# Group softmax on one core: stores moved from SyncE's ring to GpSimd's queue, loads left on SyncE's ring

One Trainium2 chip, one core. The metric is device microseconds of a whole execution, the median of several runs; a profile's span is the same execution seen from inside and is some 2 us shorter. A run is called slow here when it is over 1.5% above the fastest of its kernel. "Landing" is the moment when all sixteen completions of a transfer have arrived (the trace has 2048 of them for 128 DMAs).

## The reference

The input x is 4 x 4096 x 4352 in float32. Each row of 4352 falls into 8 groups of 544, and each group gets its own softmax:

```python
x_g = x.reshape(B, N, 8, 544)
x_g = x_g - x_g.max(axis=-1, keepdims=True)
exp = np.exp(x_g)
out = exp / exp.sum(axis=-1, keepdims=True)
```

285.2 MB are read and 285.2 MB are written.

## The kernel before

A tile is 256 rows, two per partition: 128 x 8704 numbers, 4352 KB. There are 64 tiles, five buffers, and all is done in place. VectorE takes the negated maxima of a row (eight groups at once), ScalarE eight exponentials with their sums, VectorE the reciprocals and the product. Loads and stores stand in one order on one ring, that of SyncE:

```python
def take(engine, sem, n=1):
    engine.sem_inc(sem, -n).wait_op(sem, n, "sem-ge")
# ... (row, vector_max, vector_scale, scalar_exp)
def load(t, source):
    nc.sync.dma_start(out=bufs[t % NT][:, :], in_=source).then_inc(landed[t % NT], 16)

def store(t, target):
    take(nc.sync, scaled, R)
    nc.sync.dma_start(out=target, in_=bufs[t % NT][:, :]).then_inc(stored[t % NT], 16)

def step(t, source, target):
    store(t, target)
    take(nc.sync, stored[(t - 1) % NT], 16)
    load(t + AHEAD, source)          # AHEAD = 4

for t in range(AHEAD):
    load(t, xt[t])
nc.sync.sem_inc(stored[NT - 1], 16)
with nc.sync.Fori(0, ring_turns) as u:
    for t in range(NT):
        step(t, turn_in[u, t], turn_out[u, t])
# ... (the last four tiles, and the waits for the last five stores)
```

VectorE's order: the maximum of row s+1 stands before the scaling of row s.

## Time and profile before

| | before |
|---|---|
| time, median of the first 3 runs (4 with the one beside the changed kernel) | 1329.14 us (1329.29 us) |
| span of the profiled run | 1326.8 us |
| DMA: mean over the span, steady part | 430 GB/s, 433 GB/s |
| VectorE busy | 91% |
| last store landed / end | 1325.5 us / 1326.8 us |

Two more lines of the kernel before, from the instructions at its last source lines (operation and count, then duration in ns as min/median/max, then start of the first and the last in us):

```profile
L56 SPq COMPARE_BRANCH  x1: 43/43/43, 1325.6 to 1325.6; - x1
```

```profile
L169 POOLq DRAIN  x3: 34/41/82, 0.7 to 1326.6; - x3
```

SyncE's branch at 1325.6 us comes right after its wait for the last store. The second line is GpSimd's DRAIN, an instruction of the program's fixed closing and not of the kernel's text; the longest takes 82 ns. In the packed trace the first of the three (41 ns) ran already at 0.7 us, because GpSimd has no work in this kernel; the other two (82 and 34 ns) stand at the end. Between the landing and the end lie 1.3 us.

### The profile page before, as it was taken

The numbers are of one execution on the slowest core, as the hardware profiler recorded it, in microseconds if no ns is written. First come the engines' busy times: TensorE is split into PE (matmuls) and PEld (weight loads), VectorE is DVE, ScalarE is ACT, GpSimd is POOL, SyncE is SP. The second block draws the span as 40 slices with busy tenths as digits, with TensorE's granted clock in tenths as the row PEclk, the third lists the DMA queues.
The fourth block names the chain that finished last, engine by engine and source line by source line (L and its number), as shares of the span: only waits on it lengthen the run. The fifth ranks groups of instructions, "written<-read, shape, count | busy, mean of one in ns | idle before, by whom it ended". The sixth has DMA issues, their size and how long they took to land. (4 is left out here: it accounts for less than half of the span.)

```text
span 1326.8 us, 3155 instructions
## 1 busy us (share of the span) xinstructions
DVE 1207.7 (91%) x384; ACT 764.4 (58%) x2049; POOL 0.2 (0%) x4
## 2 busy tenths in 40 slices
DVE  5999999999898898998988989889899898998984
ACT  3666565655565555655655556555565555655652
POOL 0000000000000000000000000000000000000000
DMA  9999999999999999999999999999999999999998
GB/s 403 419 431 433 429 430 430 436 433 429 431 433 436 433 431 430 435 435 436 431 431 433 436 433 433 430 432 436 435 433 429 433 436 436 431 430 433 435 435 358
DMA packets 18435, 570.46 MB, mean 430 GB/s; under 512 B 2048, under 2 KB 2048, under 8 KB 2048
## 3 DMA queue, kind: packets, MB, share of 16 engines
q1 hardware_dynamic: 18432, 570.43, 99.7%
q14 instruction: 3, 0.02, 0.0%
HBM read 285.21 MB, written 285.21 MB: 430 GB/s over the span
## 5 line engine op out<-in xcount | busy, mean ns | idle before, releaser
L82 ACT ACTIVATE xt<-xt,mx 128x544 f32<-128x544 f32 x1024 | 751.3, 734 | 539.2 <-DVE mx L63 539.2
L63 DVE TENSOR_REDUCE mx<-xt 128x8 f32<-128x4352 f32 x128 | 599.1, 4681 | 94.8 <-DMA xt<-in_x_dram 94.8
L72 DVE TENSOR_TENSOR xt<-xt,rs 128x4352 f32<-128x4352 f32 x128 | 600.6, 4692 | 4.4
L82 ACT ACTIVATION_READ_ACCUMULATOR xt<-xt,mx 128x1 f32 x1024 | 191.0, 187 | 0.0
L69 DVE RECIPROCAL rs<-sm 128x8 f32<-128x8 f32 x128 | 24.6, 193 | 2.6 <-ACT xt L82 2.6
L121 ACT ACT_TABLE_LOAD x1 | 1.3, 1283 | 0.9 <-SPq L49 0.9
L158 POOL MEMSET const-bfloat16-1.0<- 128x1 bf16 x1 | 0.1, 101 | 0.0
L158 POOL MEMSET const-uint8-127<- 128x1 uint8 x1 | 0.1, 101 | 0.0
L158 POOL MEMSET const-float32-0.0<- 128x1 f32 x1 | 0.1, 98 | 0.2 <-issue 0.2
L158 POOL MEMSET const-float32-1.0<- 128x1 f32 x1 | 0.1, 98 | 0.0
## 6 DMA issues: line engine op xcount, KB each, us to landing
xt<-in_x_dram SPq DMA_DIRECT2D x64, 4352.0 KB, 30.6
out_dram<-xt SPq DMA_DIRECT2D x64, 4352.0 KB, 40.3
```

The costliest lines, as they stand in the source:

```text
L63: i = nc.vector.reduce_max(out=mx[:, s, :], in_=row(s), axis=X, negate=True)
L69: nc.vector.reciprocal(out=rs[:, s, :], in_=sm[:, s, :]).wait_op(exp_done, s + 1, "sem-ge").then_inc(rec_done, 1)
L72: nc.vector.tensor_tensor(out=xr, in0=xr, in1=rs[:, s, :].unsqueeze(2).to_broadcast([P, G, Dg]), op=mybir.AluOpType.mult,).wait_op(rec_don ...
L82: i = nc.scalar.activation(out=xr[:, g, :], in_=xr[:, g, :], func=Exp, bias=mx[:, s, g:g + 1], scale=1.0, accum_out=sm[:, s, g:g + 1],)
L121: nc.scalar.preload_act_table(Exp)
L158: nc = _bacc.Bacc("TRN2", target_bir_lowering=False, num_devices=1)
```

## The change

Its intent: take the stores, and with them the waits for the computation, out of the order of the loads. SyncE only loads, up to five tiles ahead; GpSimd only stores, from a loop of 12 turns of five tiles and four tiles after it. The whole diff:

```diff
--- before.py
+++ after.py
@@ -19,7 +19,6 @@
     R = 2
     NT = 5
     S = R * NT
-    AHEAD = NT - 1
     xf = x.flatten_outer_dims()
     of = out.flatten_outer_dims()
     N, D = xf.shape
@@ -27,15 +26,13 @@
     nt = N // (P * R)
     nr = nt * R
     turns = (nr - 1) // S
-    ring_turns = (nt - AHEAD) // NT
+    ring_turns = nt // NT
     steps = ring_turns * NT
     f32 = mybir.dt.float32
     X = mybir.AxisListType.X
     Exp = mybir.ActivationFunctionType.Exp
     xt = xf.rearrange("(t p r) d -> t p (r d)", p=P, r=R)
     ot = of.rearrange("(t p r) d -> t p (r d)", p=P, r=R)
-    turn_in = xf[AHEAD * P * R:(AHEAD + steps) * P * R, :].rearrange(
-        "(u b p r) d -> u b p (r d)", b=NT, p=P, r=R)
     turn_out = of[:steps * P * R, :].rearrange("(u b p r) d -> u b p (r d)", b=NT, p=P, r=R)
 
     landed = [tc.alloc_semaphore(f"landed{b}") for b in range(NT)]
@@ -95,28 +92,23 @@
     def load(t, source):
         nc.sync.dma_start(out=bufs[t % NT][:, :], in_=source).then_inc(landed[t % NT], 16)
 
+    for t in range(nt):
+        if t >= NT:
+            nc.sync.wait_ge(stored[t % NT], 16 * (t // NT))
+        load(t, xt[t])
+    for t in range(nt - NT, nt):
+        nc.sync.wait_ge(stored[t % NT], 16 * (t // NT + 1))
+
+
     def store(t, target):
-        take(nc.sync, scaled, R)
-        nc.sync.dma_start(out=target, in_=bufs[t % NT][:, :]).then_inc(stored[t % NT], 16)
+        take(nc.gpsimd, scaled, R)
+        nc.gpsimd.dma_start(out=target, in_=bufs[t % NT][:, :]).then_inc(stored[t % NT], 16)
 
-    def step(t, source, target):
-        store(t, target)
-        take(nc.sync, stored[(t - 1) % NT], 16)
-        load(t + AHEAD, source)
-
-    for t in range(AHEAD):
-        load(t, xt[t])
-    nc.sync.sem_inc(stored[NT - 1], 16)
-    with nc.sync.Fori(0, ring_turns) as u:
+    with nc.gpsimd.Fori(0, ring_turns) as u:
         for t in range(NT):
-            step(t, turn_in[u, t], turn_out[u, t])
+            store(t, turn_out[u, t])
     for t in range(steps, nt):
-        if t + AHEAD < nt:
-            step(t, xt[t + AHEAD], ot[t])
-        else:
-            store(t, ot[t])
-    for t in range(nt - NT, nt):
-        nc.sync.wait_ge(stored[t % NT], 16)
+        store(t, ot[t])
 
     nc.scalar.preload_act_table(Exp)
     with nc.scalar.Fori(0, turns):
```

## The prediction

> **What bounds the kernel now.** I read the page's shares first, then the queues, then stretches of the middle and the end, then the waits and the issues in order of time. The page, busy rows and bytes:
>
> ```profile
> DVE 1207.7 (91%) x384; ACT 764.4 (58%) x2049; POOL 0.2 (0%) x4
> DMA  9999999999999999999999999999999999999998
> DMA packets 18435, 570.46 MB, mean 430 GB/s; under 512 B 2048, under 2 KB 2048, under 8 KB 2048
> q1 hardware_dynamic: 18432, 570.43, 99.7%
> ```
>
> One hardware queue carries everything, and its packets fill 99.7% of the span of 16 engines. 18432 packets are 128 DMAs (64 loads, 64 stores) of 144: 128 rows of 34816 B (two rows of x per partition) and 16 packets under 512 B[...]. VectorE is busy for 91%; the question is whether the missing 9% are waits for data or the reverse. Stretches of the steady part and of the end (columns: stretch, length, busy time and count of VectorE, ScalarE, GpSimd, TensorE clock, DMA share, GB/s):
>
> ```profile
> 300.00:400.00 100.00, 90.96 (x31) 59.63 (x160) 0.00 (x0) 1.00 1.00 432
> 700.00:800.00 100.00, 91.54 (x30) 58.18 (x157) 0.00 (x0) 1.00 1.00 433
> 1100.00:1200.00 100.00, 93.20 (x30) 58.01 (x156) 0.00 (x0) 1.00 1.00 434
> 1310.00:1320.00 10.00, 0.00 (x0) 0.00 (x0) 0.00 (x0) 1.00 1.02 439
> 1322.00:1326.80 4.80, 0.00 (x0) 0.00 (x0) 0.00 (x0) 1.00 0.08 36
> ```
>
> The share is 1.00 at 432 to 434 GB/s from 300 to 1200 us; only the last 5 us are empty. One load or store of 4352 KB is 4.456 MB, so a tile, in and out, is 8.913 MB: at 433 GB/s 20.58 us. The issues in order of time show the same period (start, length, line):
>
> ```profile
> 616.14 0.34 SPq L96 DMA_DIRECT2D xt<-in_x_dram  x1
> 616.66 0.35 SPq L100 DMA_DIRECT2D out_dram<-xt  x1
> 636.71 0.34 SPq L96 DMA_DIRECT2D xt<-in_x_dram  x1
> 637.63 0.35 SPq L100 DMA_DIRECT2D out_dram<-xt  x1
> 657.27 0.34 SPq L96 DMA_DIRECT2D xt<-in_x_dram  x1
> ```
>
> 636.71 - 616.14 = 20.57 us per tile. The median time from issue to landing is 30.6 us for a load and 40.3 us for a store, against 10.29 us (4.456 MB at 433 GB/s) for the transfer itself: three to four transfers stand in the ring at any time. So SyncE's waits cost nothing here, although they add up to 1235.5 us in the queue's own waits: they hold back an issue that would only stand in line. VectorE is what waits:
>
> ```profile
> DVE mx L63 <- DMA xt<-in_x_dram: 94.8, 51, 13.9
> ```
>
> 13.9 us of it is the first load; the other 50 waits are 80.9 us, 1.6 us each. That is its room per tile: four large instructions, 2 x (4.68 + 4.69), and two reciprocals of 0.19 less small overlaps come to 18.9 us against 20.57.
>
> The floor of this traffic: 64 x 20.57 = 1316.5 us, about 2 us until the first bytes flow and some 5 us from the last bytes to the end (the emptied stretch above) make 1324, against a span of 1326.8. No order of issue can win more than a few us.
>
> [...]
>
> **The change part by part.**
> - *Loads no longer stand behind a store's wait.* SyncE issues load t as soon as store t-5 has landed, and five loads instead of four at the start. In steady state the ring before was never empty, so this buys 0 us. At the start, load 4 was issued at 39.86 us when four loads nearly had drained: the stretch 41 to 44 us moves 371 GB/s and 44 to 54 us moves 414 GB/s. Filled to 433 that is 3 x 62/433 + 10 x 19/433 = 0.9 us. VectorE still starts on the first landing at 13.9 us. Gain: 0 to 1 us.
> - *Enough transfers stay in flight.* A tile that landed at 605.6 has its last product done at 635.7 (631.08 + 4.6): 30 us in compute, because the second row's scaling stands behind the next tile's maximum. With both rings busy each has half the rate, so a load and a store take 20.6 us each: 20.6 + 30 + 20.6 = 71 us[...]. Five buffers at one tile per 20.57 us allow 103 us. The 27 us left stand as waiting transfers in the rings[...]. Cost: 0.
> - *Stores from GpSimd.* 64 issues from a loop of 12 turns of five and four after it.[...]
> - *Side by side instead of in turns.*[...] Nothing in this trace prices that.[...]
>
> Sum: 1329.1 - 0.5[...]: 1337 us.
>
> **The rivals.**
> - *Exact tie* (1327 to 1331)[...]. For it: [...]three to four transfers waiting. Against: the tuned kernel's author bothered to put loads and stores in one order on one ring.
> - [...]
> - [...]
> - *A win from two directions at once*, if load and store use different paths and the limit of 433 is one-way[...]. Against: with only stores left (1310 to 1320 us) the rate is 439, with both kinds 433[...]. Nearly excluded.
>
> **Range and chances.** The floor leaves at most some 3 us below 1329, so the range starts at 1325[...]. A gain over 2% needs 1302.6, under the 1316.5 that the bytes alone take: 0.02. Slower by 2% needs 1355.7, a mix at under 425 GB/s[...]: 0.32. Within: 0.66.
>
> **What would show each step.** After: two queues of about 50% of the span each, summing to 98 to 100%; steady stretches at 425 to 433 GB/s; VectorE's waits for loads about 81 us plus whatever the time grew; its products still 4.69 us[...]; landings of loads and stores long against 10.3 us. A DMA share well under 1.00 with no transfer waiting would break the buffer step[...]. The prediction is wrong if the steady rate is under 425, or if VectorE loses its 1.6 us.

The forecast's sum came to 1337 us: 1329.1 us of the kernel before, less 0.5 us for the loads freed from the stores' waits, plus two terms: 1 us for stores from GpSimd and about 7.5 us for loads and stores side by side. The upper end of the range, 1388 us, rested on such a term for the same mix. Under *Enough transfers stay in flight*, an allowance of 5 us takes the 71 us to 76 and so leaves 27 of the 103.

## The result

The changed kernel takes 1333.62 us (1333.31 to 1335.02, 4 runs) against 1329.29 us of the kernel before in its 4 runs. Ratio 1.0032, with a 95% interval of 1.0015 to 1.0049: within the 2% that counts as the same, though the interval leaves 1 out. Ratios here and below are the mean time of one kernel's fast runs over that of the other's of the same rounds, so not quite the ratio of the medians.

The page of the changed kernel, queues and busy shares:

```profile
DVE 1207.9 (91%) x384; ACT 764.5 (57%) x2049; POOL 34.3 (3%) x68
q1 hardware_dynamic: 9216, 285.22, 49.7%
q0 software_dynamic: 9216, 285.22, 49.6%
xt<-in_x_dram SPq DMA_DIRECT2D x64, 4352.0 KB, 29.8
out_dram<-xt POOLq DMA_DIRECT2D x64, 4352.0 KB, 42.1
```

Two queues of half the traffic each, the same count of packets as before in all, and landings as long as before (30.6 and 40.3 us there): the transfers still stand in line. Stretches of the changed kernel (length, busy VectorE, ScalarE, GpSimd, clock, DMA share, GB/s):

```profile
41.00:44.00 3.00, 2.97 (x3) 0.33 (x1) 0.00 (x0) 1.00 1.10 371
44.00:54.00 10.00, 9.97 (x4) 6.53 (x19) 0.00 (x0) 1.00 0.96 404
300.00:400.00 100.00, 93.22 (x30) 57.68 (x155) 2.65 (x5) 1.00 1.00 433
1100.00:1200.00 100.00, 91.40 (x31) 56.60 (x153) 2.66 (x5) 1.00 1.00 433
1311.00:1314.00 3.00, 1.48 (x1) 0.00 (x0) 0.53 (x1) 1.00 0.08 35
1314.00:1325.00 11.00, 0.00 (x0) 0.00 (x0) 0.00 (x0) 1.00 0.94 405
1325.00:1331.60 6.60, 0.00 (x0) 0.00 (x0) 0.00 (x0) 1.00 0.00 0
```

The steady rate is 433 GB/s as before, so the middle of the run lost nothing. Two things are new at the end: a hole from 1311 to 1314 us, before the last store's data, and 6.6 us from the last data to the end. The instruction lines for the end, in the same view as shown for the kernel before:

```profile
L93 SPq COMPARE_BRANCH  x1: 33/33/33, 1325.1 to 1325.1; - x1
```

```profile
L161 POOLq DRAIN  x3: 34/102/5295, 1325.4 to 1331.2; - x3
```

The last store landed at 1325.1 us, even 0.5 us sooner than before. Then the first of GpSimd's three closing DRAINs ran for 5295 ns, where it took 41 ns in the kernel before (the other two took 102 and 34 ns), and all other engines waited for it at the program's closing barrier (the last DRAINs of ScalarE, VectorE and TensorE began only at 1331.0 us). It began only at 1325.4 us, although GpSimd had issued its last store at 1313.1 us: 0.3 us after SyncE's branch at 1325.1 us, which follows its wait for the last store. ScalarE's and VectorE's first DRAINs at the end began at 1325.4 us too. The queue's own waits show the same from SyncE's side (engine, line, what it waited for, us in total, times, longest), first before, then after:

```profile
SPq L169 <- PEq L169: 0.6, 2, 0.4
```

```profile
SPq L161 <- PEq L161: 5.4, 2, 5.2
```

The view names PE because PE's record came last at the barrier; the DRAIN line shows who was late. The sum closes to 0.1 us: -0.5 us at the landing, +5.2 us in the DRAIN, against spans of 1326.8 and 1331.6 us (+4.8).

### The profile page after: what moved, and what is told of

Its sections match the earlier page's. It is cut to its first block, busy times and chain, and to the rows that moved or that the text cites. A ratio compares the mean times of both kernels' runs of the same rounds, so it can differ in the third digit from the quotient of the medians.

```text
span 1331.6 us, 2987 instructions
## 1 busy us (share of the span) xinstructions
DVE 1207.9 (91%) x384; ACT 764.5 (57%) x2049; POOL 34.3 (3%) x68
## 3 DMA queue, kind: packets, MB, share of 16 engines
q1 hardware_dynamic: 9216, 285.22, 49.7%
q0 software_dynamic: 9216, 285.22, 49.6%
## 5 line engine op out<-in xcount | busy, mean ns | idle before, releaser
L60 DVE TENSOR_REDUCE mx<-xt 128x8 f32<-128x4352 f32 x128 | 599.2, 4682 | 97.5 <-DMA xt<-in_x_dram 97.5
L69 DVE TENSOR_TENSOR xt<-xt,rs 128x4352 f32<-128x4352 f32 x128 | 600.6, 4692 | 4.4
L105 POOL DMA_DIRECT2D out_dram<-xt x64 | 34.1, 533 | 1278.9 <-POOLq L53 1278.9
```

The lines of the kernel that those rows point to most:

```text
L60: i = nc.vector.reduce_max(out=mx[:, s, :], in_=row(s), axis=X, negate=True)
L69: nc.vector.tensor_tensor(out=xr, in0=xr, in1=rs[:, s, :].unsqueeze(2).to_broadcast([P, G, Dg]), op=mybir.AluOpType.mult,).wait_op(rec_don ...
L105: nc.gpsimd.dma_start(out=target, in_=bufs[t % NT][:, :]).then_inc(stored[t % NT], 16)
```

## The experiments

Theory A after the result: a closing DRAIN of 5.3 us is the price of having issued any DMA from GpSimd, whenever it was. Rival A2: it is an after-effect of the last transfer, or it grows with the number of DMAs. Rival B: the DRAIN hides a loss in the order of the last transfers or in the mix of two rings, seen in the hole at 1311 us. All twelve kernels below gave the reference's result. Their diffs are cut to the lines that matter and simplified ("..." stands for what is left out).

**One tiny DMA in the kernel before.**

```diff
+    nc.gpsimd.dma_start(out=tiny[:, :], in_=xf[0:P, 0:8]).then_inc(tiny_in, 16)
+    nc.gpsimd.wait_ge(tiny_in, 16)
```

> The kernel before with one extra GpSimd DMA of 4 KB (128 x 8 numbers of x into an unused tile) at the very start, 1.3 ms before the end. Theory A (the closing DRAIN of GpSimd takes 5.3 us instead of 0.08 us once GpSimd has issued any DMA, whenever): a closing DRAIN of about 5.3 us and 1329.3 + 5.2 = 1334.5 us. Rival A2 (it is an after-effect of a transfer that has just ended, or grows with the 64 DMAs): DRAIN about 0.1 us, 1329.3 us. Rival B (the cost is in the order of the last transfers or in the mix of the rings): also 1329.3 us.

Measured: 1329.87 us, ratio 0.9998 (0.9985 to 1.0012). GpSimd's closing DRAIN:

```profile
L173 POOLq DRAIN  x3: 40/83/125, 1327.1 to 1327.9; - x3
```

125 ns, not 5.3 us; and 1329.87 us is the time of the kernel before. Theory A falls: using the queue once does not cost it.

**Stores on ScalarE's hardware ring.** The loop of ScalarE is shifted by one row, so that it issues the store of a tile after the first exponentials of the next one, when the scaling is just done:

```diff
-        take(nc.gpsimd, scaled, R)
-        nc.gpsimd.dma_start(out=target, ...)
+        take(nc.scalar, scaled, R)
+        nc.scalar.dma_start(out=target, ...)
```

> The kernel after with its stores issued from ScalarE's hardware ring instead of GpSimd's software queue: still two rings side by side, five loads ahead, no GpSimd DMA. Theory A: DRAIN back at about 0.1 us and the last store landing as in the kernel after, about 0.5 us sooner than before: 1328.5 us (1327 to 1330). Rival B (side by side makes the last load later and the last store stand alone behind a gap): 1333 us as in the kernel after, the same gap of some 3.5 us before the last store's data. Rival C (ScalarE, blocked by its stores' waits, delays the exponentials): over 1335 us, VectorE waiting for ScalarE by more than 2.6 us.

Measured: 1327.27 us (1326.93 to 1328.09), ratio 0.9976 (0.9962 to 0.9990). Rival C is out: VectorE waited 2.6 us for ScalarE, as before. Rival B is out too. The hole is there, shallower, and so is the sooner end:

```profile
1310.00:1311.00 1.00, 1.00 (x1) 0.00 (x0) 0.00 (x0) 1.00 0.16 70
1311.00:1314.00 3.00, 1.56 (x1) 0.00 (x0) 0.00 (x0) 1.00 0.46 197
1325.00:1326.20 1.20, 0.00 (x0) 0.00 (x0) 0.00 (x0) 1.00 0.00 0
```

```profile
L163 POOLq DRAIN  x3: 34/41/82, 0.7 to 1325.9; - x3
```

Side by side as such cost nothing here (ratio 0.9976); with GpSimd's queue goes the long DRAIN (none over 82 ns, where it was 5295).

**The last store in two halves**, in the changed kernel and on the two hardware rings:

```diff
-    store(nt - 1, ot[nt - 1])
+    for r in range(R):
+        take(nc.gpsimd, scaled, 1)      # nc.scalar in the second kernel
+        nc.gpsimd.dma_start(out=ot[nt - 1][:, r * D:(r + 1) * D], ...)
```

> The kernel after with its last store in two halves, each row as soon as it is scaled: the first half can fill the gap in which the engines stand empty before the last store. If the gap costs time: last landing 3 to 4 us earlier, 1333.6 - 3.5 = 1330 us, DRAIN still 5.3 us. If the gap is no cost[...]: 1333.6 us.

> Two hardware rings and the split last store together. Theory A with a costly gap: 1328.5 - 3.5 = 1325 us, the only version under the kernel before. With a gap that costs nothing: 1328.5 us. Rival B without the drain being the cause: about 1330 us.

Measured: 1334.17 us (1.0029) and 1327.11 us (0.9974; without the split 0.9976). The first half store was there to fill the hole, and nothing came of it. In the traces a store's sixteen completions do not come together: from the first to the last it is 5.0 us in the median in the kernel before and 3.0 us in the changed one. Whether that is why the hole costs nothing is not shown; what is shown is that filling it gains nothing. And the DRAIN of the changed kernel with the split gave the new theory, 5377 ns for 65 DMAs against 5295 ns for 64:

```profile
L165 POOLq DRAIN  x3: 34/102/5377, 1326.2 to 1332.1; - x3
```

**The count.** 125, 5295 and 5377 ns for 1, 64 and 65 DMAs lie on one line: 43 ns and 82 ns for each DMA. The 41 ns for no DMA, in the kernel before, fit it too. Four kernels test it. First, 64 tiny DMAs in the kernel before, whose stores stay on SyncE:

```diff
+    for k in range(64):
+        nc.gpsimd.dma_start(out=tiny[:, 8 * k:8 * k + 8], in_=xf[0:P, 8 * k:8 * k + 8]).then_inc(tiny_in, 16)
+        nc.gpsimd.wait_ge(tiny_in, 16 * (k + 1))
```

> The kernel before with 64 GpSimd DMAs of 4 KB at the start instead of one; its stores stay on SyncE's ring. New theory (the closing DRAIN of GpSimd takes 0.04 us and 0.082 us for each DMA that GpSimd has issued since the last drain; 64 gave 5295 ns, 65 gave 5377 ns, 1 gave 125 ns): DRAIN 43 + 64 x 82 = 5.29 us, time 1329.3 + 5.2 = 1334.5 us[...]. Rival A2b (an after-effect of a large transfer that has just ended): DRAIN about 0.1 us, 1330 us. A DRAIN that goes with the packets (32 here, 144 for a store) would be near 1.2 us.

```profile
L174 POOLq DRAIN  x3: 40/96/5287, 1328.7 to 1334.5; - x3
```

5287 ns, at 43 + 64 x 82 = 5291, 850 us after the last of them; and 1337.28 us, ratio 1.0056 (1.0043 to 1.0069). The DRAIN is 5.2 us of the 7.4; the last store also landed 2.9 us later than in the kernel before, which 64 small transfers in the first 480 us, one about every 7.5 us, may account for, but this was not separated. A DRAIN by packets or bytes is out: the tiny DMAs have 32 packets each, the stores 144.

Second, the changed kernel with its last four stores on SyncE:

```diff
-    for t in range(steps, nt):
-        store(t, ot[t])
+    # on SyncE, after its loads:
+    for t in range(steps, nt):
+        nc.sync.wait_ge(scaled_last, R * (t - steps + 1))
+        nc.sync.dma_start(out=ot[t], in_=bufs[t % NT][:, :]).then_inc(stored2[t % NT], 16)
```

> The kernel after with its last four stores from SyncE's ring: GpSimd's last DMA lies some 50 us before the end. Count theory: DRAIN 43 + 60 x 82 = 4.96 us, time 1333.3 us. Rival A2b (recency): DRAIN about 0.1 us and 1328.5 us.

```profile
L166 POOLq DRAIN  x3: 34/107/4968, 1325.7 to 1331.2; - x3
```

4968 ns for 60 DMAs (4.96 expected), and 1333.16 us, ratio 1.0022 (1.0009 to 1.0035). The after-effect of a recent transfer is out.

Third, a drain in each turn of the changed kernel:

```diff
         for t in range(NT):
             store(t, turn_out[u, t])
+        nc.gpsimd.drain()
```

> The kernel after with a drain of GpSimd after the fifth store of each of the 12 turns, while GpSimd waits anyway. Count theory, with the drain clearing the count: closing DRAIN 43 + 4 x 82 = 0.37 us; each inner one waits some 42 us for the store before it, holding the next store back by some 21 us, which the 27 us of waiting transfers absorb: 1333.6 - 4.9 = 1328.7 us. If the hold empties the engines: 12 times up to 10 us more, over 1340 us. If the cost goes with the whole run's DMAs: closing DRAIN 5.3 us still, 1333.6 us.

```profile
L110 POOLq DRAIN  x12: 32581/43647/44237, 115.2 to 1256.7; - x12
```

```profile
L162 POOLq DRAIN  x3: 46/102/376, 1346.5 to 1347.4; - x3
```

The closing DRAIN is 376 ns for the four DMAs since the last inner one, as expected (0.37): the 60 DMAs ahead of the inner drains no longer count. But the time is 1348.36 us, ratio 1.0127 (1.0107 to 1.0146), and my 1328.7 us was wrong. An inner drain waits for the store just issued, 43.6 us in the median, and holds the next store back. Ten turns from the second drain on took 104.7 us each, against 5 x 20.57 = 102.9 us, and VectorE's last product ended at 1332 us instead of 1312 us. My second forecast, engines emptied and over 1340 us, has the time but not the reason. The page:

```profile
q1 hardware_dynamic: 9216, 285.22, 50.4%
q0 software_dynamic: 9216, 285.22, 49.1%
```

The two queues fill 99.5% of the longer span, as they filled 99.3% in the changed kernel, and the stretches of 100 us from 200 to 1300 us have a DMA share of 0.99 to 1.01 at 421 to 429 GB/s. So the engines did not stand empty: the loads' packets took longer, 1325 ns in the mean after 200 us against 1288 ns in the changed kernel. Summed over the run and shared among 16 engines, packets took 18 us more than in the changed kernel, of some 21 us that were lost (16 us in the span, and 5 us that the shorter closing DRAIN won). Why a held-back store does this is not shown.

One thing was left untried. Each inner drain ended 0.25 us after the landing it waited for, though five DMAs at 43 + 5 x 82 ns would be 0.45 us. Why is not shown, and whether a single drain right after the issue of the last store would cost less than 5.3 us was not run.

Fourth, twice as many DMAs for the same bytes, one per row:

```diff
+        for r in range(R):
+            take(nc.gpsimd, scaled, 1)
+            nc.gpsimd.dma_start(out=target[:, r * D:(r + 1) * D], ...)
```

> The kernel after with every store in two, one per row: 128 GpSimd DMAs with the same bytes and twice the rows of half the length. Count theory: DRAIN 43 + 128 x 82 = 10.54 us, 1333.6 + 5.2 = 1338.8 us, and a little more if the shorter packets of 17408 B cost something (two of 646 ns seen for one of 1288: 0.3%, 2 us on the half of the traffic). By bytes: DRAIN 5.3 us still, 1334 to 1336 us.

Measured: 1423.01 and 1404.55 us in its two fast runs, 1439 to 1451 us in four that were slow, so no interval. The DRAIN missed too:

```profile
L163 POOLq DRAIN  x3: 40/102/1870, 1418.5 to 1420.9; - x3
```

By the same line 1870 ns would be about 22 DMAs, not 128. GpSimd stood idle once, for 15.3 us ahead of a store, in no wait that the profile shows; a later kernel, with pairs of half stores from GpSimd, has one such idle time too (2.6 us) and the same 1870 ns. Why the line fails at 128 DMAs is not shown. It holds up to 65 here.

**The loss by half-length stores** (5.6 and 7.0% in the two fast runs) bears on the mix. The same half stores, issued in pairs when the tile is done, from GpSimd and from ScalarE:

```diff
         take(nc.gpsimd, scaled, R)      # nc.scalar in the second kernel
-        nc.gpsimd.dma_start(out=target, in_=bufs[t % NT][:, :])...
+        for r in range(R):
+            nc.gpsimd.dma_start(out=target[:, r * D:(r + 1) * D], ...)
```

> After all_split (1440 us where 1339 was expected): the kernel after with every store as two GpSimd DMAs, one per row, but both issued together when the tile is scaled. If packets of 17408 B in the software queue beside loads of 34816 B are what slows the engines: 1400 to 1450 us again. If it was the row-by-row issue that changed the order of the transfers: about 1339 us. The closing DRAIN: 1.9 us as in all_split[...].

> The same pairs of half stores from ScalarE's hardware ring. If the software queue is the cause of all_split's loss: 1327 to 1335 us. If it is the unequal packets of the two rings, whoever issues them: 1400 us and more.

Measured: 1399.63 us, ratio 1.0517 (1.0492 to 1.0543), closing DRAIN 1870 ns again; and 1397.28 us (1385.84 to 1407.80; one of its four runs, the profiled one, was slow), ratio 1.0473 (1.0408 to 1.0539). The software queue is not the cause. Then both sides in halves on two hardware rings, and half stores on the one ring of the kernel before:

```diff
-    nc.sync.dma_start(out=bufs[t % NT][:, :], in_=source)...
+    for r in range(R):
+        nc.sync.dma_start(out=bufs[t % NT][:, r * D:(r + 1) * D], in_=source[:, r * D:(r + 1) * D])...
```

> Two hardware rings with loads and stores both in halves: packets of 17408 B in both. If it is the inequality of the packets in the two rings that cost 5%: equal again, 1327 to 1335 us (648 ns for half a row's pair against 1288/2 = 644: +0.6% at most). If shorter packets in themselves cost it once two rings share the engines: 1400 us or more.

> The kernel before, one ring in order, with every store as two halves: unequal packets without two rings. If it takes two rings side by side for the loss: 1329 to 1337 us (the 4 ns more per half packet and a second set of completion packets). If short stores in themselves cost it: 1380 us or more.

Measured: 1335.13 us, ratio 1.0038 (1.0021 to 1.0055), and 1334.52 us, ratio 1.0033 (1.0016 to 1.0050). With both sides in halves a packet of 17408 B took about 649 ns in the mean (99.9% of 16 engines' span of 1333.2 us, over 32768 packets), half of a whole one being 644. Stretches of two of these kernels, unequal packets from two queues (pairs of half stores from GpSimd), then equal ones (both sides in halves):

```profile
200.00:300.00 100.00, 90.81 (x30) 56.20 (x151) 5.31 (x10) 1.00 1.00 427
700.00:800.00 100.00, 86.84 (x28) 53.68 (x144) 5.28 (x10) 1.00 0.99 410
1200.00:1300.00 100.00, 85.61 (x28) 53.09 (x143) 4.26 (x8) 1.00 0.99 405
```

```profile
700.00:800.00 100.00, 90.03 (x29) 56.05 (x152) 0.00 (x0) 1.00 1.01 431
1200.00:1300.00 100.00, 90.73 (x30) 55.93 (x152) 0.00 (x0) 1.00 1.01 431
```

The engines are as busy, by share, but late in the run they move 5% less. In the unequal case a load's packet of 34816 B takes 1379 ns in the mean after 200 us, where it takes 1288 ns in the changed kernel. The median is 1288 ns in both: the loss sits in a minority of packets (15% of the loads' packets took over 1400 ns, against 0.0%). Nor is it there from the start: 427 GB/s from 200 to 300 us became 405 to 410, with the same packets.

Unequal packets on one ring cost 0.3%, half packets in both of two rings 0.4%; unequal packets in two rings cost 5%. So of these kernels only the last combination loses much. It is not the only way to long packets, though: the drain in each turn has them with equal ones (6% over 1400 ns). The reverse case, short loads beside long stores, was not run. Why some packets take longer, and why late, stays open.

## Why the prediction was right, and where not

The range (1325 to 1388) and the class hold, and 1337 is 3.4 us above the measurement. But that nearness is luck: 7.5 us for the mix did not come, and 5.2 us came that no term had. Term by term:

- *The bound*: right. 433 GB/s and a share of 1.00 before and after. The floor read the end wrongly: the stretch to 1326.8 us was not 5 us after the last bytes. The last packet ended at 1325.1 us, so the floor is nearer to 1320 than to 1324 us.
- *Loads freed from the stores' waits, 0 to 1 us at the start*: 0. The stretch from 44 to 54 us moves 404 GB/s with the fifth load already in the ring, against 414 before. The dip that I read as a ring running dry is there with a fuller ring too, so the ring was not its cause.
- *Five buffers and 27 us of waiting transfers*: right for the steady state. Two rings had half the rate each, as assumed (49.7% and 49.6% of the span for half the bytes each). The allowance of 5 us was an estimate: in the kernel before the first data began 1.0 us after the first issue, and the last landing came 0.35 us after the last packet, 2.7 us for two transfers. VectorE's waits for loads are 97.5 us against 94.8. Even with a store held back for 44 us, in the kernel with a drain in each turn, the engines stayed full (a share of 0.99 to 1.01); what was lost there was lost in longer packets.
- *Stores from GpSimd, 1 us in the sum*: this step failed. It took the issue of a DMA for the queue's whole price. That part is small: the last store's data began 1.10 us after the start of its issue on GpSimd's queue and 0.85 us after it on ScalarE's ring, and in all the last store landed 0.5 us sooner than before, not later. What the queue cost stood elsewhere, after the last landing: 64 x 82 ns in the closing DRAIN, 5.2 us, for which the prediction had no term.
- *The mix, about 7.5 us in the sum*: 0. The stores on ScalarE's ring show side by side at no loss, even 0.24% under the kernel before. A larger loss did not come either, with equal packets in the two rings. Losses of some 60 to 90 us came only with half-length stores beside whole loads, for a reason that stays open.
- *VectorE beside stores from GpSimd*: nothing came of it; its products are 600.6 us in total before and after, 4692 ns each.

The best version is the one with two hardware rings, 1327.27 us: 0.24% under the kernel before in the same rounds, inside the 2% that counts as a tie. Where that gain lies was not tested apart.

## What to carry to other kernels

With the DMA engines full (a share of 1.00), moving transfers to another queue changed the ends of the run here, and not its middle (433 GB/s before and after), as long as the packets stayed as they were: read the profile from the last landing to the last instruction, closing included, before and after. The DMAs on GpSimd's queue were paid at the end, 82 ns each here up to 65 of them; the same stores on ScalarE's hardware ring had no DRAIN over 82 ns at the end, 0.24% under the kernel before instead of 0.32% over it. If loads and stores run side by side on two rings, try packets of one length first: here they ran at a ratio of 0.9976 (whole) and 1.0038 (both in halves), unequal ones at 1.0473 and 1.0517.
